# Claiming the tiles of the late chunks' unrounded copies early, and putting the third product ahead of the fourth in two feed-forward units

## The chip, the cores and the metric

The kernel runs on one core of one Trainium2 chip. The metric is the device time of one execution in microseconds (us). Five engines work side by side, each through its own instructions in order: TensorE (PE in the profile, with its weight loads as PEld), VectorE (DVE), ScalarE (ACT), GpSimd (POOL) and SyncE (SP). DMA transfers are issued by the engines' queues; here SP issues plain weight loads, and POOL issues loads that add onto what already lies in the tile.

## The reference

The kernel computes a trunk of two layers for 512 tokens of width 1024, in float32. Layer 0 is a spatial-gating mixer, layer 1 a retention mixer with four heads; behind each mixer stands a SwiGLU feed-forward of hidden width 2816:

```
def swiglu(h, w_gu, w_down):
    a, b = jnp.split(h @ w_gu, 2, axis=-1)
    return (jax.nn.silu(a) * b) @ w_down

for i in range(DEPTH):
    hn = rmsnorm(h, mix_norm_g[i])
    if i % N_MIXERS == 0:
        h = h + sgu_mixer(hn, ...)
    else:
        h = h + retention(hn, positions, ...)
    h = h + swiglu(rmsnorm(h, ffn_norm_g[i]), ffn_w_gu[i], ffn_w_down[i])
return rmsnorm(h, final_norm_g)
```

## The kernel before

**Numbers.** Every float32 product is made of three TensorE products of reduced form (`three`, L246 to L249): high half by high half, low by high, high by low. So each operand is split first. ScalarE writes the rounded high half of a weight tile (`wh_...`, L216), VectorE the remainder (`wl_...`, L223). The raw weights (`wr_...`, 512 KB a tile) come by DMA, from SP (L346) or, added onto a tile, from POOL (L349).

**Products.** The large matrix products use a scheme of seven block products instead of eight (`seven`), named P1, P7, P6, Q4, P5, P2, P3. They add up in three accumulators in PSUM: X takes P1, P6, P5, P3 one after the other, Y takes P7 and then Q4, Z takes P2. PSUM has four slots, handed out in turn. In a feed-forward unit ScalarE copies intermediate states of an accumulator (L1026): X after P1 to `s`, Y after P7 to `y`, X after P6 to `u`. Only after that copy may P5 add onto X. After P5 VectorE adds X to `y`, and only then may P3 go on. Behind Q4 VectorE adds Y to `u`, ScalarE takes its silu, and VectorE multiplies it with `y`; behind P3 VectorE multiplies X with the gated `s`.

**Stages.** Layer 0's mixer (until about 165 us), its feed-forward f0, the retention layer (names ending in `_r`; it starts at about 500 us), and its feed-forward f1 (from about 870 us). A feed-forward is six units of the up and gate product (`gu`), with a first half of the down product (`dn_0`) behind units 0 and 1, and the rest at the end. Tokens come in four chunks of 128. Chunks 2 and 3 are normalised and turned first, and the work of the next stage starts on them; chunks 0 and 1 come late. Of the turned activations the kernel keeps the rounded halves (`XH`, `XL`) and an unrounded copy `xr`, in two pairs of tiles: `XR[name, 1]` for chunks 2 and 3, `XR[name, 0]` for chunks 0 and 1. `raw_copy` writes them on ScalarE (L704) from the accumulator `xT`; sums and differences of them are the operands of P7, P6, P5 and P3 (`xA`: L727, L740, L743). All of these tiles come from one pool of 38 buffers, handed out in the order of the requests.

**Order.** `opened` queues the first four steps of units 0 and 1 in turn with the late chunks' work, and the rest of unit 0 behind them. The order of the products in a unit is a table: FIRST for units 0 and 1, LATER for units 2 to 5 (L314 to L317). The order of the single instructions on each engine is then set by a scheduler that weighs a model of their durations, so a table also moves instructions that it does not name.

Of the kernel before, what the change touches and what calls it, by code (L numbers as in the profile page):

```python
# [8 lines left out]
F32 = mybir.dt.float32  # L9
# [6 lines left out]
P = 128  # L16
# [95 lines left out]
def trunk(ctx, tc, x, positions, mix_g, ffn_g, fin_g, sgu_w_in, sgu_w_s, sgu_b_s, sgu_ln_g, sgu_ln_b,  # L112
          sgu_w_out, ret_w_in, ret_gn_g, ret_w_out, ffn_w_gu, ffn_w_down, invf, decay, out):
    nc = tc.nc
# [9 lines left out]
    H = T // 2  # L124

    def G(name, dtype=F32, shape=(P, 2, T)):
        return gen.tile(list(shape), dtype, tag="g", name=name)
# [10 lines left out]
    def PS(name, shape=(P, 2, T)):  # L138

        s = ps_free.pop(0)  # L140
        t = psp.tile(list(shape), F32, tag=f"ps{s}", name=name)
        ps_held.append((t, s))
        return t

    def done(*tiles):

        for t in tiles:
            i = next(i for i, (u, _) in enumerate(ps_held) if u is t)
            ps_free.append(ps_held.pop(i)[1])
# [102 lines left out]
    X = xpool.tile([P, NC, D], F32, name="X")  # L252
# [60 lines left out]

    ORDER = ("P1", "P7", "P6", "Q4", "P5", "P2", "P3")  # L314
    LATER = ("P1", "P7", "P6", "P2", "P5", "Q4", "P3")
    FIRST = ("P1", "P2", "P7", "P6", "P5", "Q4", "P3")
    SPREAD = ("P1", "P7", "P6", "P2", "Q4", "P5", "P3")  # L317
    BLOCKS = {"P1": ("11",), "P7": ("22", "12"), "P6": ("22", "12", "11"), "Q4": ("22", "12", "11", "21"),
              "P5": ("12", "11"), "P2": ("21",), "P3": ("22",)}
# [2 lines left out]
    def seven(name, w, groups, c1, c2, A, evac, mid=None, look=3, turned=False, order=ORDER, dma=(), onto=(),  # L322
# [10 lines left out]
        chain = {"P1": "X", "P7": "Y", "P6": "X", "Q4": "Y", "P5": "X", "P2": "Z", "P3": "X"}  # L333
# [3 lines left out]
        acc = {}  # L337
# [89 lines left out]
        def run(i):  # L427
            p, (g, s, nk) = order[i // len(steps)], steps[i % len(steps)]
            if apart and p == "P3" and i % len(steps) == 0:
                acc.update({("W", c): PS(f"W{c}_{name}") for c in range(2)})  # L430
            elif p in opens and i % len(steps) == 0:
                acc[chain[p]] = PS(f"{chain[p]}_{name}", (P, wide // P, H) if turned else (P, 2, T))
            if s == 0:
                j = asks.index((p, g))
                for q in asks[j:j + (1 if order is FIRST and p in FIRST[:2] or tied and i == 0 else look)]:
                    A(*q, ask=True)
            n = i % len(steps)
            if p != order[-1]:
                for c in range(2):
                    with tc.issue_after(xn["turned"].ins) if (p, n) in tied and c == 0 else nullcontext():  # L440
                        matmuls(p, g, s, nk, c)
                if n == len(steps) - 1:
                    evac(p, acc, None)
                    if p in closes:
                        done(acc[chain[p]])
            elif n < len(steps) - by_chunk:
                for c in range(2):
                    matmuls(p, g, s, nk, c)
            elif n == len(steps) - 1:
                for c in range(2):  # L450
                    with tc.issue_after(mm.ins) if apart and c == 1 else nullcontext():
                        for st_ in steps[-by_chunk:]:
                            mm = matmuls(p, *st_, c)
                    evac(p, acc, c)
                    if apart:
                        done(acc["W", c])
                if not apart:
                    done(acc["X"])
            if mid and (p, n) in mid:
                mid[p, n]()  # L460

# [233 lines left out]
    XR = {}  # L695

    def raw_copy(name):

        def copy(c, ps):
            if (name, c // 2) not in XR:  # L700
                XR[name, c // 2] = [G(f"xr_{name}_{c // 2}_{j}", F32, (P, 4, H)) for j in range(2)]
            cs = slice((c % 2) * P, (c % 2 + 1) * P)
            for j in range(2):
                nc.scalar.activation(XR[name, c // 2][j][:, :, cs], ps[:, 4 * j:4 * j + 4, :], AF.Copy)  # L704
        return copy
# [296 lines left out]
    def feed_forward(l, ready):  # L1002

        w = ffn_w_gu[l]
        hq = [[None, None] for _ in range(5)]
        he = []
        gates = [None] * 6

        def hidden(u, i):
            gates[u].finish()  # L1010
            return hq[u][i]

        def hidden_end(part, i):
            gates[4].finish()
            gates[5].finish()
            return he[part][i][:, 0:3, :]

        xparts = xA(f"f{l}")

        def unit(u, mid=None, order=LATER, tied=()):  # L1020
            st_ = {}
            n = 2 if u == 5 else 4

            def copy(key, src):
                st_[key] = G(f"{key}_{l}_{u}", F32, (P, 4, H))[:, 0:n, :]
                nc.scalar.activation(st_[key], src, AF.Copy)  # L1026

            def product(i, r, g, ms):
                if u < 4:
                    parts = [(hq[u][i][:, ms, :], ms)]  # L1030
                elif u == 4:
                    parts = [(he[a][i][:, 0:2, :], slice(2 * a, 2 * a + 2)) for a in range(2) if ms.start <= 2 * a < ms.stop]
                else:
                    parts = [(he[a][i][:, 2, :], a) for a in range(2)]
                for dst, ms in parts:
                    nc.vector.scalar_tensor_tensor(dst, r[:, ms, :], -1.0, g[:, ms, :], ALU.mult, ALU.mult)

            def evac(p, acc, c):
                if p == "P7":
                    copy("y7", acc["Y"])  # L1040
                    if u < 4:
                        hq[u][0] = st_["y7"]
                elif p == "P1":
                    copy("s1", acc["X"])
                    if u < 4:
                        hq[u][1] = st_["s1"]
                elif p == "P6":
                    copy("u2", acc["X"])
                elif p in ("Q4", "P2"):
                    a, ps = (st_["u2"], acc["Y"]) if p == "Q4" else (st_["s1"], acc["Z"])  # L1050
                    gates[u] = Chain(lambda: nc.vector.tensor_tensor(a, a, ps, ALU.add),  # L1051
                          lambda: nc.scalar.activation(a, a, AF.Silu),
                          *([lambda: product(0, st_["y7"], a, slice(0, n))] if p == "Q4" else []))
                elif p == "P5":
                    nc.vector.tensor_tensor(st_["y7"], st_["y7"], acc["X"], ALU.add)
                    if u == 5:
                        he.extend([[G(f"he{l}_{a}_{i}", F32, (P, 4, H)) for i in range(2)] for a in range(2)])
                elif p == "P3" and n == 4:
                    product(1, acc["X"], st_["s1"], slice(2 * c, 2 * c + 2))
                elif c == 1:  # L1060
                    product(1, acc["X"], st_["s1"], slice(0, 2))
            first = order is FIRST
            c1, wide = (u * T, T) if u < 5 else (20 * P, 2 * P)
            return seven(f"gu{l}_{u}", w, rows(0, KD), c1, FF + c1, xparts, evac, mid, turned=True, order=order,
                         dma=("P7", "P5") if u == 0 else ("P7",), onto=("P6", "Q4") if u == 0 else ("Q4",) if u < 5 else (),
                         tied=tied, early=0 if u < 5 else 2, wide=wide)

        t = [list(range(4 * u, 4 * u + 4)) for u in range(5)]
        A = [combos(f"h{l}_0", lambda g, i, j: hidden(j, 1 - i), (4,)),
             combos(f"h{l}_1", lambda g, i, j: hidden_end(j, i) if g else hidden(2 + j, i), (4, 3))]  # L1070

        def asks(A):
            return {("P2", 1): lambda: A("P1", 0, ask=True), ("P5", 0): lambda: A("P7", 0, ask=True), ("P3", 1): lambda: A("P6", 0, ask=True)}

        one = unit(0, order=FIRST)
        two = unit(1, {("P7", 1): lambda: A[0]("P1", 0, ask=True), ("P5", 0): lambda: A[0]("P7", 0, ask=True), ("P3", 1): lambda: A[0]("P6", 0, ask=True)},
                   order=FIRST, tied=(("P1", 0),))
        opened(one, two, xparts)
        jobs.extend(two[4:])
        into_x(f"dn{l}_0", ffn_w_down[l], [(t[0], t[1])], A[0], halves=(1, 0))  # L1080
        jobs.extend(unit(2, {**{(p, 0): turn_tables for p in LATER}, ("P3", 1): turn_tables} if l == 0 else None))
        jobs.extend(unit(3))
        jobs.extend(unit(5))
        jobs.extend(unit(4, asks(A[1])))
        into_x(f"dn{l}_1", ffn_w_down[l], [(t[2], t[3]), ([16, 17, 20], [18, 19, 21])], A[1], ready, look=5, apart=ready is finish)
# [157 lines left out]
    t = [list(range(4 * hd, 4 * hd + 4)) for hd in range(HEADS)]  # L1243
    into_x("ro", ret_w_out[0], [(t[0], t[1]), (t[2], t[3])], outA, normed("f1", ffn_g[1:2], raw_copy("f1")),
           {("P1", 1): heads[3][3], ("P7", 1): heads[3][2]})


    feed_forward(1, finish)
    pipeline(jobs)

# [32 lines left out]
```

## Time and profile before

| | |
|---|---|
| device time, median of 3 runs | 1201.62 us (1200.46 to 1202.15) |
| the profiled execution's own time | 1203.81 us |
| its span | 1202.1 us |
| TensorE busy | 1181.7 us (98%), 7158 matmuls |
| VectorE busy | 941.1 us (78%) |
| ScalarE busy | 650.6 us (54%) |
| POOL busy | 163.2 us (14%) |
| DMA traffic | 219.56 MB, 183 GB/s over the span |
| granted TensorE clock, mean | 0.997 |

A row of the timeline has the start in us, the duration in us, the engine, the line of the code, the operation, the tiles written and read, their shapes, and in brackets how long the engine was idle before it and what ended that. Numbers of buffers are left out of names, so `wr_gu_P` is any raw tile of a P product. A duration of a pipelined matmul overlaps that of the next: the spacing of the starts tells what one costs. A row of the windows has the window, its length, then busy time and count of instructions for PE, PEld, DVE, ACT and POOL, the granted clock, the DMA share and the GB/s. A row of the waits has the waiting instruction, what ended the wait, the sum in us, how many times, and the longest.

### The profile page before, as it was taken

How to read it: one execution, taken by the hardware profiler on the slowest of the kernel's cores; microseconds unless marked ns; L12 is line 12 of the kernel's file. 1: busy time of each engine (PE TensorE's matmuls, PEld its weight loads, DVE VectorE, ACT ScalarE, POOL GpSimd, SP SyncE). 2: the span in 40 equal slices, each digit the busy share in tenths (PEclk: the TensorE clock that was granted, in tenths of full speed). 3: DMA queues.
4: the chain of work that ended last, by engine and by line, in shares of the span. 5: the costliest groups of instructions: out<-in, count | busy, mean ns of one | idle time of the engine just before them, and what ended most of it. 6: DMA issues, size and time to landing. Idle time of an engine off the chain costs nothing.

```text
span 1202.1 us, 17966 instructions
## 1 busy us (share of the span) xinstructions
PE 1181.7 (98%) x7158; PEld 1059.7 (88%) x7158; DVE 941.1 (78%) x1119; ACT 650.6 (54%) x821; POOL 163.2 (14%) x145
## 2 busy tenths in 40 slices
PE   8999999999999999999999999999999999999997
PEld 7888899989999987988888888888889989999985
DVE  5587998899977789787665757889787996676897
ACT  5523775554444547555554645576575555535465
POOL 1000122111010130111101011220121110101210
PEclk9999999999999999999999999999999999999999
DMA  9912878898674888767557457778878788856892
GB/s 310 286 41 64 240 160 188 222 233 207 157 204 111 227 177 277 173 145 188 110 167 148 132 128 170 193 145 275 223 159 215 152 228 216 206 128 195 165 246 97
DMA packets 122020, 219.56 MB, mean 183 GB/s; under 512 B 7464, under 2 KB 23888, under 8 KB 121936
## 3 DMA queue, kind: packets, MB, share of 16 engines
q1 hardware_dynamic: 85872, 150.23, 37.7%
q0 software_dynamic: 35776, 67.66, 33.6%
q8 instruction: 56, 0.92, 0.3%
q10 hardware_dynamic: 288, 0.52, 0.1%
q14 instruction: 28, 0.23, 0.1%
HBM read 215.24 MB, written 2.10 MB: 181 GB/s over the span
## 4 chain that ended last, share of the span: by engine, by line
PE 85%; DMA 5%; issue 4%; DVE 2%; ACT 2%; POOL 1%; SPq 0%; DVEq 0%; POOLq 0%; ACTq 0%
PE X_gu L247 6%; PE X_gu L249 6%; PE X_gu L248 6%; PE Y_gu L249 3%; PE Y_gu L248 3%; PE Y_gu L247 3%; DMA wr_gu_P<-in_ffn_w_gu 3%; PE X_dn L247 3%; PE X_dn L248 3%; PE X_dn L249 3%; PE X_vg L248 2%; PE X_vg L247 2%; PE X_vg L249 2%; PE ps_qk L247 2%; PE ps_qk L248 2%
## 5 line engine op out<-in xcount | busy, mean ns | idle before, releaser
L216 ACT ACTIVATE wh_gu_P<-wr_gu_P 128x1024 fp32r<-128x1024 f32 x132 | 135.3, 1053 | 82.2 <-DVE wr_gu_P L377 51.0
L223 DVE TENSOR_TENSOR wl_gu_P<-wr_gu_P,wh_gu_P 128x1024 fp32r<-128x1024 f32 x132 | 158.7, 1221 | 22.2 <-ACT wh_gu_P L216 22.1
L349 POOL DMA_DIRECT2D wr_gu_P<-in_ffn_w_gu x50 | 60.8, 1238 | 411.9 <-DVE wl_gu_P L223 180.0
L216 ACT ACTIVATE wh_dn_P<-wr_dn_P 128x1024 fp32r<-128x1024 f32 x72 | 69.0, 980 | 41.3 <-DMA wr_dn_P<-in_ffn_w_down 17.5
L223 DVE TENSOR_TENSOR wl_vg_P<-wr_vg_P,wh_vg_P 128x1024 fp32r<-128x1024 f32 x48 | 58.5, 1223 | 36.4 <-ACT wh_vg_P L216 30.2
L223 DVE TENSOR_TENSOR wl_dn_P<-wr_dn_P,wh_dn_P 128x1024 fp32r<-128x1024 f32 x72 | 79.7, 1130 | 3.5 <-PE Y_gu L248 2.2
L349 POOL DMA_DIRECT2D wr_vg_P<-in_ret_w_in x26 | 31.5, 1249 | 261.6 <-DMA wr_vg_P<-in_ret_w_in 90.8
L216 ACT ACTIVATE wh_vg_P<-wr_vg_P 128x1024 fp32r<-128x1024 f32 x48 | 49.7, 1055 | 26.7 <-DMA wr_vg_P<-in_ret_w_in 14.6
L349 POOL DMA_DIRECT2D wr_dn_P<-in_ffn_w_down x36 | 41.9, 1200 | 146.5 <-DMA wr_dn_P<-in_ffn_w_down 45.5
L248 PE MATMUL ps_qk<-XL_r,wh_qk 128*128 128x512 f32 (+1 forms) x160 | 55.6, 348 | 0.0
L247 PE MATMUL ps_qk<-XH_r,wh_qk 128*128 128x512 f32 (+1 forms) x160 | 55.4, 349 | 0.0
L249 PE MATMUL ps_qk<-XH_r,wl_qk 128*128 128x512 f32 (+1 forms) x160 | 54.9, 347 | 0.0
L247 PE MATMUL X_gu<-XH_f,wh_gu_P 128*128 128x256 f32 x176 | 50.7, 288 | 2.2 <-ACT xr_f L704 2.2
L247 PE MATMUL Z_gu<-XH_f,wh_gu_P 128*128 128x256 f32 x176 | 50.0, 284 | 1.4 <-DVE s L1051 1.4
L249 PE MATMUL Y_gu<-XH_f,wl_gu_Q 128*128 128x256 f32 x176 | 49.9, 284 | 0.8 <-DVE wl_gu_Q L223 0.8
L249 PE MATMUL X_gu<-XH_f,wl_gu_P 128*128 128x256 f32 x176 | 50.5, 287 | 0.0
L248 PE MATMUL X_gu<-XL_f,wh_gu_P 128*128 128x256 f32 x176 | 50.5, 287 | 0.0
L247 PE MATMUL X_gu<-xP5h_f,wh_gu_P 128*128 128x256 f32 x176 | 49.9, 284 | 0.5 <-ACT u L1026 0.5
L247 PE MATMUL X_gu<-xP6h_f,wh_gu_P 128*128 128x256 f32 x176 | 49.9, 284 | 0.5 <-ACT xP6h_f L740 0.5
L247 PE MATMUL Y_gu<-XH_f,wh_gu_Q 128*128 128x256 f32 x176 | 49.9, 284 | 0.2 <-ACT wh_gu_Q L216 0.2
L249 PE MATMUL Z_gu<-XH_f,wl_gu_P 128*128 128x256 f32 x176 | 49.9, 283 | 0.0
L248 PE MATMUL X_gu<-xP6l_f,wh_gu_P 128*128 128x256 f32 x176 | 49.8, 283 | 0.0
(580 smaller groups left out, 4145.1 us busy)
## 6 DMA issues: line engine op xcount, KB each, us to landing
wr_gu_P<-in_ffn_w_gu SPq DMA_DIRECT2D x110, 512.0 KB, 5.4
wr_gu_P<-in_ffn_w_gu POOLq DMA_DIRECT2D x50, 512.0 KB, 7.2
wr_dn_P<-in_ffn_w_down SPq DMA_DIRECT2D x50, 512.0 KB, 5.1
wr_vg_P<-in_ret_w_in SPq DMA_DIRECT2D x40, 512.0 KB, 4.8
wr_dn_P<-in_ffn_w_down POOLq DMA_DIRECT2D x30, 512.0 KB, 6.9
wr_vg_P<-in_ret_w_in POOLq DMA_DIRECT2D x26, 512.0 KB, 7.2
wr_ro_P<-in_ret_w_out SPq DMA_DIRECT2D x20, 512.0 KB, 5.3
wr_qk<-in_ret_w_in SPq DMA_DIRECT2D x32, 256.0 KB, 3.1
```

What stands on the lines that cost most here:

```text
L216: nc.scalar.activation(h, s, AF.Copy)
L223: nc.vector.tensor_tensor(l, s, f32(h), ALU.subtract)
L247: nc.tensor.matmul(o, ah, bh, start=start, stop=False, skip_group_check=True)
L248: nc.tensor.matmul(o, ah, bl, start=False, stop=False, skip_group_check=True)
L249: return nc.tensor.matmul(o, al, bh, start=False, stop=stop, skip_group_check=True)
L349: nc.gpsimd.dma_start(raw[p, 0, g, s][:, 0:nk, :], source(b, g, s, nk), accum_op=ALU.add)
```

## The change

FIRST gets P3 ahead of Q4. With that, P3 is no longer the last product of units 0 and 1: its gate product is one VectorE operation over 128x1024 instead of two over half of that, Q4 becomes the product that is worked off chunk by chunk, with its add, silu and multiplication once behind the second half, and the request for the down product's P6 operand moves from the end of P3 to the end of Q4. `raw_copy` asks for both pairs of `xr` tiles at its first call in a layer (chunk 3), and POOL writes one column of zeros into each of the two tiles that chunks 0 and 1 will fill. That is done in f0, r and f1: six fills. The values that the fills write are overwritten later.

```diff
-    FIRST = ("P1", "P2", "P7", "P6", "P5", "Q4", "P3")
+    FIRST = ("P1", "P2", "P7", "P6", "P5", "P3", "Q4")
...
                 if not apart:
-                    done(acc["X"])
+                    done(acc[chain[p]])
...
         def copy(c, ps):
-            if (name, c // 2) not in XR:
-                XR[name, c // 2] = [G(f"xr_{name}_{c // 2}_{j}", F32, (P, 4, H)) for j in range(2)]
+            if (name, 0) not in XR:
+                for i in (1, 0):
+                    XR[name, i] = [G(f"xr_{name}_{i}_{j}", F32, (P, 4, H)) for j in range(2)]
+                for t in XR[name, 0]:
+                    nc.gpsimd.memset(t[:, 0, 0:1], 0.0)
...
                 elif p == "P6":
                     copy("u2", acc["X"])
+                elif p == "Q4" and c == 0:
+                    pass
                 elif p in ("Q4", "P2"):
...
-                elif p == "P3" and n == 4:
+                elif c is None:
+                    product(1, acc["X"], st_["s1"], slice(0, n))
+                elif n == 4:
                     product(1, acc["X"], st_["s1"], slice(2 * c, 2 * c + 2))
...
-        two = unit(1, {..., ("P3", 1): lambda: A[0]("P6", 0, ask=True)},
+        two = unit(1, {..., ("Q4", 1): lambda: A[0]("P6", 0, ask=True)},
                    order=FIRST, tied=(("P1", 0),))
```

The order of the instructions moves as follows at the places that the prediction speaks of. In the names, `gu1_0` is unit 0 of f1 and `dn1_0` the first down product of f1, and the last number tells one buffer from another.

The first place is TensorE in f1's unit 0, from P6's last matmuls on. Before:

```order
L247 MATMUL X_gu1_0_8019<-xP6h_f1_8208,wh_gu1_0_P6_0_2_8244 128x256
L248 MATMUL X_gu1_0_8019<-xP6l_f1_8209,wh_gu1_0_P6_0_2_8244 128x256
L249 MATMUL X_gu1_0_8019<-xP6h_f1_8208,wl_gu1_0_P6_0_2_8245 128x256
L247 MATMUL Y_gu1_0_8315<-XH_f1_7855,wh_gu1_0_Q4_0_0_8371 128x256
L248 MATMUL Y_gu1_0_8315<-XL_f1_7856,wh_gu1_0_Q4_0_0_8371 128x256
L249 MATMUL Y_gu1_0_8315<-XH_f1_7855,wl_gu1_0_Q4_0_0_8372 128x256
```

With the change:

```order
L247 MATMUL X_gu1_0_8025<-xP6h_f1_8212,wh_gu1_0_P6_0_2_8248 128x256
L248 MATMUL X_gu1_0_8025<-xP6l_f1_8213,wh_gu1_0_P6_0_2_8248 128x256
L249 MATMUL X_gu1_0_8025<-xP6h_f1_8212,wl_gu1_0_P6_0_2_8249 128x256
L247 MATMUL X_gu1_0_8025<-xP5h_f1_8285,wh_gu1_0_P5_0_0_8280 128x256
L248 MATMUL X_gu1_0_8025<-xP5l_f1_8286,wh_gu1_0_P5_0_0_8280 128x256
L249 MATMUL X_gu1_0_8025<-xP5h_f1_8285,wl_gu1_0_P5_0_0_8281 128x256
```

Q4's matmuls stood between P6 and P5 (32 of them here, 26 in f0's unit 0, 30 and 45 in the two units 1); now none stands there in the two units 0, and two in each unit 1.

The second place is ScalarE in f0's opening, where the turned chunks are rounded and copied. Before:

```order
L671 ACTIVATE XH_f0_1264<-xT_f0_0_1453 128x8x128
L216 ACTIVATE wh_gu0_1_P2_0_2_1447<-wr_gu0_1_P221_0_2_1388 128x1024
L671 ACTIVATE XH_f0_1264<-xT_f0_1_1529 128x8x128
L704 ACTIVATE xr_f0_0_0_1464<-xT_f0_0_1453 128x4x128
L704 ACTIVATE xr_f0_0_1_1465<-xT_f0_0_1453 128x4x128
L216 ACTIVATE wh_gu0_0_P7_0_0_1494<-wr_gu0_0_P722_0_0_1314 128x1024
```

With the change (L707 is what was L704):

```order
L671 ACTIVATE XH_f0_1264<-xT_f0_0_1457 128x8x128
L216 ACTIVATE wh_gu0_1_P2_0_2_1451<-wr_gu0_1_P221_0_2_1392 128x1024
L671 ACTIVATE XH_f0_1264<-xT_f0_1_1531 128x8x128
L216 ACTIVATE wh_gu0_0_P7_0_0_1496<-wr_gu0_0_P722_0_0_1318 128x1024
L707 ACTIVATE xr_f0_0_0_1270<-xT_f0_0_1457 128x4x128
L707 ACTIVATE xr_f0_0_1_1271<-xT_f0_0_1457 128x4x128
```

The rounding of P7's first weight tile has moved ahead of the two unrounded copies. On TensorE, unit 1's P1 (accumulator `X_gu0_1`) has moved ahead of unit 0's P2 (`Z_gu0_0`) there.

The third place is TensorE in f1's first down product, from the end of P2 on. Before:

```order
L248 MATMUL Z_dn1_0_9083<-wl_dn1_0_P2_0_2_8998,h1_0_P2h_0_9003 128x512
L249 MATMUL Z_dn1_0_9083<-wh_dn1_0_P2_0_2_8997,h1_0_P2l_0_9004 128x512
L247 MATMUL X_dn1_0_8962<-wh_dn1_0_P5_0_0_9019,h1_0_P5h_0_9040 128x512
L248 MATMUL X_dn1_0_8962<-wl_dn1_0_P5_0_0_9020,h1_0_P5h_0_9040 128x512
L247 MATMUL Y_dn1_0_9002<-wh_dn1_0_Q4_0_0_9056,h1_0_Q4h_0_9084 128x512
```

With the change:

```order
L248 MATMUL Z_dn1_0_9085<-wl_dn1_0_P2_0_2_9000,h1_0_P2h_0_9005 128x512
L249 MATMUL Z_dn1_0_9085<-wh_dn1_0_P2_0_2_8999,h1_0_P2l_0_9006 128x512
L247 MATMUL Y_dn1_0_9004<-wh_dn1_0_Q4_0_0_9058,h1_0_Q4h_0_9086 128x512
L248 MATMUL Y_dn1_0_9004<-wl_dn1_0_Q4_0_0_9059,h1_0_Q4h_0_9086 128x512
L247 MATMUL X_gu1_2_9242<-XH_f1_7857,wh_gu1_2_P1_0_0_9145 128x256
L248 MATMUL X_gu1_2_9242<-XL_f1_7858,wh_gu1_2_P1_0_0_9145 128x256
L247 MATMUL X_dn1_0_8964<-wh_dn1_0_P5_0_0_9021,h1_0_P5h_0_9042 128x512
```

Two Q4 matmuls of the same product and two P1 matmuls of unit 2 now stand ahead of P5. In the retention layer the third weight tile of P7 (`wh_vg_P7_0_2`) has moved on ScalarE ahead of the rounding of chunk 1 (`XH_r`).

More of the change, by code (lines that the diff above doesn't have):

```diff
@@ L1075, in feed_forward @@
         one = unit(0, order=FIRST)
[L1076 removed]
+        two = unit(1, {("P7", 1): lambda: A[0]("P1", 0, ask=True), ("P5", 0): lambda: A[0]("P7", 0, ask=True), ("Q4", 1): lambda: A[0]("P6", 0, ask=True)},
                    order=FIRST, tied=(("P1", 0),))
```

## The prediction

> **What bounds the kernel now.** I read the first part of the page, then the chain of waits that ended last, then TensorE's waits grouped by what ended them, then its timeline at each of them.
>
> ```profile
> span 1202.1 us, 17966 instructions
> PE 1181.7 (98%) x7158; PEld 1059.7 (88%) x7158; DVE 941.1 (78%) x1119; ACT 650.6 (54%) x821; POOL 163.2 (14%) x145
> PE 85%; DMA 5%; issue 4%; DVE 2%; ACT 2%; POOL 1%; SPq 0%; DVEq 0%; POOLq 0%; ACTq 0%
> ```
>
> TensorE works for 1181.7 of 1202.1 us, and 85% of the last-ending chain is its own matmuls. No matmul is removed. The change can therefore win only what TensorE still idles, and loses every idle microsecond it adds. These are the waits that the touched places hold:
>
> ```profile
> PE xT_in L667 <- DMA X<-in_x: 3.1, 1, 3.1
> PE X_gu L247 <- ACT xr_f L704: 2.2, 1, 2.2
> PE Z_gu L247 <- DVE s L1051: 1.4, 1, 1.4
> ...
> PE Y_gu L249 <- DVE wl_gu_Q L223: 0.8, 1, 0.8
> ...
> PE X_gu L247 <- ACT u L1026: 0.5, 1, 0.5
> ...
> PE Y_vg L249 <- DVE xP7l_r L743: 0.5, 1, 0.5
> ```
>
> The first lies at the start of the program, out of the change's reach. The second is the opening of the second feed-forward layer (f1), the third that of the first (f0), the next two are f0's unit 0, and the last is the opening of the retention layer (r). Together they are 5.4 us: that is nearly all there is to win, apart from the clock, of which more below.
>
> **The change part by part.** *1. Third product ahead of the fourth, f0, unit 0.* P6's last matmul, the first Q4 matmuls and P5's first, on TensorE:
>
> ```profile
> 190.12 0.28 PE L249 MATMUL X_gu<-xP6h_f,wl_gu_P 128*128 128x256 f32 x1
> 190.60 0.38 PE L247 MATMUL Y_gu<-XH_f,wh_gu_Q 128*128 128x256 f32 x1 [0.20 <-ACT wh_gu_Q L216]
> 191.86 0.39 PE L249 MATMUL Y_gu<-XH_f,wl_gu_Q 128*128 128x256 f32 x1 [0.76 <-DVE wl_gu_Q L223]
> ...
> 195.50 0.38 PE L247 MATMUL X_gu<-xP5h_f,wh_gu_P 128*128 128x256 f32 x1 [0.51 <-ACT u L1026]
> ```
>
> ```profile
> 190.50:195.40 4.90, 3.63 (x26) 3.22 (x26) 0.00 (x0) 0.00 (x0) 1.00 1.09 230
> ```
>
> The windows row counts 26 Q4 matmuls between them. Back to back, the matmuls of this shape start 0.12 us apart (the f1 rows of part 3: 901.54 and 901.66), so 26 of them are 3.1 us of the 5.4 from 190.12 to 195.50. The other 2.27 us are the three waits and the slower matmul behind each. The change takes the Q4 matmuls away from here, and P5 stands directly behind P6. But P5 adds onto X, and ScalarE must have copied X to `u` first. The comparison point is P5's start had the Q4 matmuls cost only their own work: 195.50 - 3.12 = 192.38, from which 2.27 has still to come off or be kept. ScalarE's queue:
>
> ```profile
> 187.24 1.05 ACT L1052 ACTIVATE s<-s 128x1024 f32<-128x1024 f32 x1
> 188.19 1.01 ACT L1026 ACTIVATE y<-Y_gu 128x1024 f32<-128x1024 f32 x1
> ...
> 194.45 1.00 ACT L1026 ACTIVATE u<-X_gu 128x1024 f32<-128x1024 f32 x1
> ```
>
> The changed order puts one weight rounding ahead of the `y` copy and one more, with P3's operand, between it and the `u` copy. ScalarE starts its 1024-column operations 0.95 us apart (187.24 to 188.19): four of them from 188.19 put the `u` copy at 191.99, and P5 at 193.05. From TensorE's side, P6 ends 0.6 us later than now (part 2), so the copy ends at 190.12 + 0.6 + 0.28 + 0.05 + 1.0 = 192.05, and P5 starts at 192.1. Against 192.38, parts 1 and 2 in f0's unit 0 are between -0.3 and +0.8 (the high end with the slower first matmul, 0.1). I take **+0.3**, the middle, for neither row decides which queue is later.
>
> *2. f0's opening.* The changed ScalarE order also puts a P7 weight ahead of the two copies to `xr`:
>
> ```profile
> 164.69 1.02 ACT L671 ACTIVATE XH_f<-xT_f 128x1024 fp32r<-128x1024 f32 x1 [0.69 <-PE xT_f L667]
> 165.61 1.08 ACT L704 ACTIVATE xr_f<-xT_f 128x512 f32<-128x512 f32 x2
> 166.57 1.07 ACT L216 ACTIVATE wh_gu_P<-wr_gu_P 128x1024 fp32r<-128x1024 f32 x1
> ```
>
> ```profile
> 167.12 0.36 PE L247 MATMUL Z_gu<-XH_f,wh_gu_P 128*128 128x256 f32 x1 [1.41 <-DVE s L1051]
> ```
>
> The copies then end at 166.57 + 1.08 = 167.65. Unit 1's P1 now stands first on TensorE, in the accumulator that these copies empty, and starts at about 167.7 instead of 167.12: +0.6, which is already inside part 1. The gap grows from 1.41 to 2.0 us.
>
> *3. The other three places where P5 follows P6.* In f1's unit 0 (and, by the orders, f1's unit 1 and f0's unit 1) the Q4 matmuls that stood there hid the copy entirely:
>
> ```profile
> 901.54 0.28 PE L249 MATMUL X_gu<-xP6h_f,wl_gu_P 128*128 128x256 f32 x1
> 901.66 0.28 PE L247 MATMUL Y_gu<-XH_f,wh_gu_Q 128*128 128x256 f32 x1
> ```
>
> P6's last matmul, the copy and P5's first now run one after the other: 0.28 + 0.05 + 1.00 + 0.05 = 1.38 us from start to start (the copy as in its row of f0; 0.05 from its end at 195.45 to P5 at 195.50, taken for both handovers) where 0.12 stood, **+1.26** in f1's unit 0. Each unit 1 keeps two Q4 matmuls between, 0.24 us of cover: **+1.02** in f1 and **+1.02** in f0. I see no way for the copy to be shorter than its row, and nothing else stands between on TensorE, whose order is fixed. Were the copy queued behind another ScalarE operation, each would cost up to 0.95 more.
>
> *4. f1's down-projection after units 0 and 1.* The changed order puts two Q4 matmuls of the down-projection and two of unit 2's P1 between its P2 and its P5. Unit 2's first weights are late for that:
>
> ```profile
> 963.90 0.39 PE L249 MATMUL X_dn<-wh_dn_P,h_P6l 128*128 128x512 f32 x1
> 964.12 0.39 PE L247 MATMUL Z_dn<-wh_dn_P,h_P2h 128*128 128x512 f32 x1
> ...
> 969.34 0.39 PE L249 MATMUL Z_dn<-wh_dn_P,h_P2l 128*128 128x512 f32 x1
> ```
>
> ```profile
> 971.13 1.06 ACT L216 ACTIVATE wh_gu_P<-wr_gu_P 128x1024 fp32r<-128x1024 f32 x1 [2.02 <-DMA wr_gu_P<-in_ffn_w_gu]
> ```
>
> ```profile
> 964.32 0.37 SPq L346 DMA_DIRECT2D wr_gu_P<-in_ffn_w_gu  x1
> ```
>
> ```profile
> wr_gu_P<-in_ffn_w_gu SPq DMA_DIRECT2D x110, 512.0 KB, 5.4
> ```
>
> SyncE issues the load once P6's last matmul has ended (964.32). The weight is rounded from 971.13 to 972.19. TensorE leaves P2 at 969.57 (one spacing of 0.23 behind 969.34), and two matmuls later, at 970.03, waits until about 972.2: 2.2 us, with P5 and all that follows queued behind. At the page's median of 5.4 us a load that starts at 964.32 would be there at 969.7 and the wait would be 0.9 us; had it come before 969, nothing. I take **+2.0**, near this place's own rows, bounds 0 and 2.2.
>
> *5. The early claim.* Six one-column fills on POOL (two in each layer) are the price:
>
> ```profile
> 852.20 1.22 POOL L349 DMA_DIRECT2D wr_gu_P<-in_ffn_w_gu  x1 [44.52 <-DMA wr_gu_P<-in_ffn_w_gu]
> ```
>
> POOL idles 44.52 us ahead of f1's first accumulating load, and works 14% of the span, so the fills cost nothing there. Without that cover each would be bounded by this row's 1.22 us. As to the gain, in f1's opening ScalarE's order is the same as now:
>
> ```profile
> 873.34 1.05 ACT L216 ACTIVATE wh_gu_P<-wr_gu_P 128x1024 fp32r<-128x1024 f32 x1
> 874.28 0.60 ACT L704 ACTIVATE xr_f<-xT_f 128x512 f32<-128x512 f32 x1
> ```
>
> The copy starts 0.94 us behind the weight rounding ahead of it, with no idle in brackets: it waited for its turn, not for a buffer, and I count **0** for the claim here. In r's opening a weight rounding moves up into idle time of ScalarE, ahead of the second turned half, and P7's low half should come in time:
>
> ```profile
> 519.76 0.50 PE L249 MATMUL Y_vg<-wh_vg_P,xP7l_r 128*128 128x512 f32 x1 [0.46 <-DVE xP7l_r L743]
> ```
>
> That is **-0.5** (0 to -0.6).
>
> *6. The remaining edits* (P3's gate product in one operation instead of two, Q4's once instead of never split, the hook moved) change VectorE's work by less than one issue a unit; VectorE is idle 22% of the span and their results are used only by the down-projection, whose P1 and P7 stand ahead. I count 0; without that cover, one of the 0.9 to 1.2 us operations.
>
> Sum: 0.3 + 1.02 + 1.26 + 1.02 + 2.0 - 0.5 = **+5.1 us**. Against the profiled execution's own 1203.81 us (its span of 1202.1 and 1.7 around it) that gives 1208.9; that execution was 2.2 us above the median of the runs, 1201.62, so the forecast is **1206.7**. With every part at its bounds the sum goes from -0.3 + 3.3 + 0 - 0.6 = +2.4 to 0.8 + 3.3 + 2.2 - 0 = +6.3.
>
> **The clock.** One gap cost more than itself:
>
> ```profile
> 877.40:880.80 3.40, 3.40 (x19) 3.40 (x18) 2.86 (x3) 3.39 (x4) 0.13 (x1) 0.50 0.00 0
> ```
>
> A microsecond after f1's 2.2 us gap the granted clock was 0.50 for 3.4 us, in which half the work, 1.7 us, was lost. No such stretch followed f0's gap of 1.41. [...]
>
> **The rivals.** *First, the new gaps drop the clock as f1's did.* f0's opening (2.0 us) and the down-projection (2.2 us) come near the gap that did. For it: that row. Against: one case only, and f0's lost nothing at 1.41. One drop gives 1206.7 + 1.7 = 1208.4, two 1210.1. *Second, unit 2's weight arrives in time,* because the shifted program starts its load earlier or against less traffic. For it: the page's 5.4 us median against some 6.7 here. It takes off 1.1 to 2.0, and with f0 at its low end gives 1204.1 to 1205.6. *Third, the claim does free the openings.* If what delays the `xr` copies in f1 is their buffer, decided before the weight rounding in front of them, f1's gap and its slow stretch go: 5.1 - 2.2 - 1.7 = +1.2, 1202.8. If f0's gap of 1.41 goes as well and unit 2's weight is in time, the sum loses that, part 2's 0.6 and part 4: 1.2 - 1.4 - 0.6 - 2.0 = -2.8, **1198.8**, faster than now. It decides when the copies run before the weight roundings; the unbroken ScalarE rows and the unchanged order at f1 speak against it. That the claim does nothing is part of the forecast.
>
> **How the numbers follow.** Forecast 0.48; clock drops 0.12; weight in time 0.18; f1's opening freed 0.10; both openings freed 0.12. A measurement of this kernel tells 0.2%, 2.4 us, from no change. Slower: 0.48 + 0.12 + half of 0.18 (its low half lies at the bound) = 0.69. Same: 0.09 + 0.10 = 0.19. Faster: 0.12. The likeliest's own range is 1204.0 to 1207.9; to leave out 2 in 10, it goes down to 1200.0, with part of the last case outside, and up to 1209.8, with two clock drops outside.
>
> **What would show it.** Right: in the changed profile waits of some 1.0 us for `u` in four places (three of them new), a wait of up to 2.2 us for `wh_gu_P` in f1's down-projection, the waits for `wl_gu_Q` and `wh_gu_Q` gone, `xr` waits of about 2 us in both openings. Wrong: no `xr` wait at f1 or a granted clock of 1.00 throughout (third rival); `u` waits under 0.5 us; an added slow stretch near 170 or 972 us (first).

## The result

The changed kernel takes 1214.26 us (median of 4 runs, 1213.14 to 1214.98) against 1201.88 us before (1200.46 to 1203.27): a ratio of 1.0100, 95% interval 1.0088 to 1.0113. It is 12.4 us slower. The forecast was 5.1 us slower, 1206.7, at most 1209.8: the direction was right and the size less than half of what came. The profiled execution of the change took 1213.14 us, that of before 1203.81.

The page after, its first two lines, and TensorE's waits grouped by what ended them (sum in us, times, longest):

```profile
span 1211.4 us, 17975 instructions
PE 1183.4 (98%) x7158; PEld 1061.9 (88%) x7158; DVE 941.3 (78%) x1115; ACT 649.6 (54%) x821; POOL 163.7 (14%) x151
```

```profile
PE X_gu L247 <- ACT u L1029: 5.6, 4, 2.7
PE X_gu L247 <- ACT xr_f L707: 4.1, 2, 2.2
...
PE X_gu L247 <- ACT wh_gu_P L216: 3.1, 2, 1.8
...
PE ps_qk L247 <- DVE u L1172: 0.4, 1, 0.4
```

TensorE has the same 7158 matmuls and is busy 1.7 us longer. Of the four waits for `u` three are new (f0's unit 0 had one), and so are the two for unit 2's first weight (`wh_gu_P`); `xr_f` now holds both openings, where f0's wait stood under `s`. The waits for Q4's weights and for `xP7l_r` are gone. In the timeline, in order of time: f0's opening, P5 in f0's unit 1, unit 2's weight in f0's down product, P6's last matmul and P5's first in f1's unit 0, P5 in f1's unit 1, and unit 2's weight in f1's down product:

```profile
167.77 0.39 PE L247 MATMUL X_gu<-XH_f,wh_gu_P 128*128 128x256 f32 x1 [1.97 <-ACT xr_f L707]
223.82 0.39 PE L247 MATMUL X_gu<-xP5h_f,wh_gu_P 128*128 128x256 f32 x1 [0.88 <-ACT u L1029]
264.60 0.38 PE L247 MATMUL X_gu<-XH_f,wh_gu_P 128*128 128x256 f32 x1 [1.25 <-ACT wh_gu_P L216]
903.32 0.28 PE L249 MATMUL X_gu<-xP6h_f,wl_gu_P 128*128 128x256 f32 x1
906.32 0.38 PE L247 MATMUL X_gu<-xP5h_f,wh_gu_P 128*128 128x256 f32 x1 [2.72 <-ACT u L1029]
937.97 0.39 PE L247 MATMUL X_gu<-xP5h_f,wh_gu_P 128*128 128x256 f32 x1 [0.88 <-ACT u L1029]
979.31 0.39 PE L247 MATMUL X_gu<-XH_f,wh_gu_P 128*128 128x256 f32 x1 [1.81 <-ACT wh_gu_P L216]
```

The idle time at each place, in us, from two profiles of before and three of the change (two of these five are the ones shown; the others were taken with the experiments):

| place | before | changed |
|---|---|---|
| f0 opening | 1.4, 1.4 | 2.0, 2.0, 2.0 |
| f0 unit 0, P6 to P5 | 1.5, 2.6 | 1.1, 1.1, 1.1 |
| f0 unit 1, P6 to P5 | 0 | 0.9, 0.9, 0.9 |
| f0 down product, unit 2's weight | 0 | 1.3, 1.1, 1.2 |
| r opening, `xP7l_r` | 0.5, 0.5 | 0 |
| r, `ps_qk` for `u` (L1172) | 0 | 0.4, 0.9, 0.9 |
| f1 opening | 2.2, 2.2 | 2.2, 2.2, 2.2 |
| f1 unit 0, P6 to P5 | 0 | 2.7, 2.5, 3.0 |
| f1 unit 1, P6 to P5 | 0 | 0.9, 0.9, 0.9 |
| f1 down product, unit 2's weight | 0 | 1.8, 1.8, 1.8 |

By the means this is +7.3 us, and the pages agree. The spans of the three profiled executions of the change are 1211.4, 1209.0 and 1213.2 us, those of before 1202.1 and 1201.7: by the means 9.3 us more. TensorE's busy time is 2.0 us of that (1183.5 against 1181.6), and the idle time the other 7.3.

The busy time grew with the clock. In some stretches of 3.41 us the granted clock was 0.50. On both sides of the end of one, at 910.03 us:

```profile
909.02 0.41 PE L248 MATMUL X_gu<-xP5l_f,wh_gu_P 128*128 128x256 f32 x1
909.23 0.41 PE L249 MATMUL X_gu<-xP5h_f,wl_gu_P 128*128 128x256 f32 x1
...
910.30 0.28 PE L249 MATMUL X_gu<-xP5h_f,wl_gu_P 128*128 128x256 f32 x1
910.42 0.28 PE L247 MATMUL X_gu<-xP5h_f,wh_gu_P 128*128 128x256 f32 x1
```

The matmuls start 0.21 us apart at clock 0.50 and 0.12 behind it (medians 0.213 and 0.120 for this shape, at every such stretch between the program's first 20 us and its end, in all profiles of this study). So a stretch in which TensorE never idles costs 3.41 x (1 - 0.120 / 0.213) = 1.5 us by these spacings, not the 1.7 that a clock of 0.50 over 3.41 us comes to. Leaving out the first 20 us and the end of the program, the three profiles of the change hold three, one and three stretches, the two of before one each. That is 1.3 more by the means, or 2.0 us, as much as the busy time grew.

The medians of all runs lie 12.1 us apart (1214.26 over 10 runs of the changed kernel, 1202.11 over 74 of before). The other 2.8 us are open: the profiled executions of before took 1.3 and 1.7 us more than their median, those of the change 1.3 less than theirs by the mean, and no trace shows what the other executions held. One slow stretch more or less would be of that size. The mean granted clock on record, 0.9934 over these 10 runs and 0.9964 over these 74, points the same way but doesn't give the size. It counts the slow start of the program only in some runs: the eight matmuls into `xT_in` from 8.90 us before and from 9.54 us with the change took 1.94 us each time, at a recorded clock of 1.00 in one and 0.50 in the other. And among the 74, the runs at 0.995 and those at 0.997 took the same time, 1202.5 and 1202.4 us by the means.

### The profile page after: what moved, and what is told of

The parts are those of the page before. It is cut to its first block, busy times and chain, and to the rows that moved or that the text cites. A ratio compares the mean times of both kernels' runs of the same rounds, so it can differ in the third digit from the quotient of the medians.

```text
span 1211.4 us, 17975 instructions
## 1 busy us (share of the span) xinstructions
PE 1183.4 (98%) x7158; PEld 1061.9 (88%) x7158; DVE 941.3 (78%) x1115; ACT 649.6 (54%) x821; POOL 163.7 (14%) x151
## 4 chain that ended last, share of the span: by engine, by line
PE 89%; DMA 4%; DVE 3%; ACT 2%; issue 2%; SPq 0%; POOL 0%; DVEq 0%; ACTq 0%; POOLq 0%
PE X_gu L247 7%; PE X_gu L249 7%; PE X_gu L248 7%; PE Y_gu L249 3%; PE Y_gu L248 3%; PE Y_gu L247 3%; PE X_dn L248 3%; PE X_dn L247 3%; PE X_dn L249 3%; PE ps_qk L247 2%; PE ps_qk L249 2%; PE ps_qk L248 2%; PE X_vg L247 2%; PE X_vg L248 2%; PE X_vg L249 2%; DMA wr_gu_P<-in_ffn_w_gu 2%
## 5 line engine op out<-in xcount | busy, mean ns | idle before, releaser
L249 PE MATMUL X_gu<-xP5h_f,wl_gu_P 128*128 128x256 f32 x176 | 50.5, 287 | 0.0
L248 PE MATMUL X_gu<-xP5l_f,wh_gu_P 128*128 128x256 f32 x176 | 50.5, 287 | 0.0
L249 PE MATMUL Y_gu<-xP7h_f,wl_gu_P 128*128 128x256 f32 x176 | 49.8, 283 | 0.0
```

Of the source, the lines that this page charges most:

```text
L248: nc.tensor.matmul(o, ah, bl, start=False, stop=False, skip_group_check=True)
L249: return nc.tensor.matmul(o, al, bh, start=False, stop=stop, skip_group_check=True)
```

## The experiments

**Claim and order apart.** `claim_only` has the new `raw_copy` with the old FIRST, `order_only` the new FIRST with the old `raw_copy`.

```diff
 # claim_only, against the kernel before
-            if (name, c // 2) not in XR:
-                XR[name, c // 2] = [G(...) for j in range(2)]
+            if (name, 0) not in XR:
+                for i in (1, 0):
+                    XR[name, i] = [G(...) for j in range(2)]
+                for t in XR[name, 0]:
+                    nc.gpsimd.memset(t[:, 0, 0:1], 0.0)
```

> The early claim with its fills, the products in the old order. Theory A: f0's opening gap grows from 1.4 to 2.0 us as in the changed kernel (+0.6, and +1.7 where a slow stretch follows), r's opening gains 0.7, unit 0's fourth product still waits: 1201 to 1203 us, no difference that can be measured. Rival B: the claim carries half of the loss, 1206 us or more.

> P3 ahead of Q4 as in the change, but the xr tiles asked for as before, no fills. Theory A, the table's order carries nearly all of the loss: waits for u in four places (5.6 us in sum, 2.7 in f1's unit 0), waits for unit 2's first weight in both down products (1.3 and 1.8), a gap of 1.4 us in f0's opening as before: 1209 to 1212 us. Rival B, the early claim of two more buffers a layer delays the weight loads and carries half or more: at most 1207 us, u waits the same but the waits in the down products gone.

`claim_only` took 1203.22 us, ratio to before 1.0011 (1.0001 to 1.0020); `order_only` 1213.08 us, 1.0091 (1.0074 to 1.0107). The two add up, 1.3 and 10.9 us, to what the whole change costs, and the order carries nine tenths of it. Both medians lie above the ranges expected, by 0.2 and 1.1 us. TensorE's waits in `claim_only`, and then in `order_only`:

```profile
PE X_gu L247 <- ACT xr_f L707: 4.1, 2, 2.2
...
PE X_gu L247 <- ACT u L1029: 1.2, 2, 0.8
```

```profile
PE X_gu L247 <- ACT u L1026: 6.5, 4, 3.0
...
PE X_gu L247 <- ACT wh_gu_P L216: 2.7, 2, 1.5
PE X_gu L247 <- ACT xr_f L704: 2.2, 1, 2.2
PE Z_gu L247 <- DVE s L1053: 1.4, 1, 1.4
```

The longer f0 opening (1.97 us of the 4.1) belongs to the claim, the waits for `u` and for unit 2's weight to the order. That the claim holds back loads and carries half of the loss (rival B) is out: the down products wait without it too. The claim has one cost of its own, the 0.7 us that `ps_qk` waits for `u` in r: `claim_only` has that wait, `order_only` doesn't. And the claim did not shorten f1's opening, for which the third rival of the prediction had hoped.

**Unit 2's weight.** `unit2_tied` moves on TensorE only the two P1 matmuls of unit 2, in each layer, behind P5 of the down product.

```diff
+                    after_ins = xn["turned"].ins if (p, n) in tied and c == 0 else \
+                        xn["dn_mm"].ins if (p, n) == ("P1", 0) and name[:2] == "gu" and name[-2:] == "_2" and c == 0 else None
+                    with tc.issue_after(after_ins) if after_ins is not None else nullcontext():
+                        mm = matmuls(p, g, s, nk, c)
+                    if p == "P5" and name[:2] == "dn":
+                        xn["dn_mm"] = mm
```

> The changed kernel, but unit 2's P1 is not issued before the last P5 matmul of the first down products; on TensorE only these four matmuls (two in each layer) move. Theory A: both waits for wh_gu_P in the down products go (1.3 + 1.8 us, and a slow stretch behind the second in those runs that have it), nothing takes their place, 3 to 4 us less than the changed kernel of the same call: about 1210.5. Rival: the late weight is wanted by something else anyway, or the loads of the down product are late too, and the wait moves behind P5: less than 1 us gained.

It took 1210.04 us, 1.0065 (1.0051 to 1.0079), against 1214.37 of the changed kernel beside it: 4.3 us less. No wait for `wh_gu_P` is left in its list. That is a little above the 3.1 us of idle time and the 3 to 4 expected, which the spread of the runs allows.

**The changed kernel again, and the clock.**

> The changed kernel once more, for its spread and a second profile. Its gaps of TensorE in the first profile were 1.97 us (f0 opening), 2.2 (f1 opening), 2.72 (f1 unit 0), 1.81 (f1 down product), 1.25 (f0 down product); a stretch of 3.4 us at clock 0.50 followed the first three. Theory C, the clock looks at fixed windows of 3.41 us and drops for the next one where TensorE idled more than about half of one: the same gaps come back within 0.2 us, but which of the 1.8 to 2.2 us gaps are followed by a slow stretch changes with where the windows fall, so runs of the same kernel differ by steps of 1.7 us, and 1213 to 1215 us here. Rival: a gap above a fixed length always drops the clock; then the same three gaps are followed by slow stretches again and the fourth never is.

> The changed kernel, a third profile. The first two (1213.1 and 1210.7 us) account for 7.5 us of waits at full clock and 3 us of clock against 12 measured. Theory C: gaps at the same seven places within 0.3 us of the first two, and slow stretches behind those that fill more than about 1.75 us of one window. Rival: another place with more than 1 us of loss that both earlier profiles missed.

These took 1214.37 us (1210.68 to 1215.43; 1.0104, 1.0089 to 1.0119) and 1213.69 us. The gaps came back within 0.3 us at f1's unit 0 and within 0.13 elsewhere, but for `ps_qk` (0.4, then 0.9 twice); the slow stretches did not: three in the first profile, one in the second, three in the third. The windows view (start and end in us, length, PE busy and matmuls, granted clock, DMA share, GB/s) for the first profile of the change, each pair a stretch of 3.41 us and the one behind it, on the grid that the starts of the slow stretches set (169.34, 879.31 and 906.62 us in this profile: 709.97 and 27.31 us apart, 208 and 8 times 3.413):

```profile
165.93:169.34 3.41, 1.57 (x13) 1.00 0.97 253
169.34:172.75 3.41, 3.41 (x18) 0.50 0.18 13
875.90:879.31 3.41, 1.24 (x11) 1.00 0.50 91
879.31:882.72 3.41, 3.41 (x19) 0.50 0.48 151
903.21:906.62 3.41, 0.69 (x6) 1.00 1.11 199
906.62:910.03 3.41, 3.41 (x18) 0.50 1.10 255
978.30:981.70 3.40, 2.39 (x11) 1.00 1.00 225
981.70:985.10 3.40, 3.40 (x16) 1.00 1.10 190
```

And for the second:

```profile
163.99:167.40 3.41, 1.44 (x12) 1.00 1.08 222
167.40:170.81 3.41, 3.41 (x18) 0.50 0.23 87
877.37:880.78 3.41, 1.72 (x14) 1.00 0.70 148
880.78:884.19 3.41, 3.41 (x30) 1.00 0.21 82
```

The gap of f1's opening was 2.17 us in both profiles. In the first it lay whole in one window and a slow stretch followed; in the second only 1.69 us of it fell into the window from 877.37, and none followed. Over all 14 profiles of this study, but for the first 20 us and the end, TensorE idled 1.84 us or more in 18 windows at a clock of 1.00, and each was followed by a window at 0.50 (in the first profile of the change those with 1.84, 2.17 and 2.72 us, in the second the one with 1.97). No window at 1.00 with 1.70 or less was (1.01 in the first, 1.69 in the second); of four between 1.75 and 1.80, one was (1.75 in `order_only`, from 189.18 us, but not 1.79 in `unit2_tied`, from 163.30). In one case (`one_less`, from 905.96) the slow window itself idled 0.8 us and a second slow one followed it. So in these runs the time depended on where the windows fell: behind the same gap of 2.17 us TensorE's work took 1.5 us longer in the first profile and no longer in the second. That is what theory C expected, and the rival (a fixed length of gap) is out.

What a stretch costs the program can be less. In all three profiles of the change P5 in f0's unit 0 starts 25.9 us behind the opening's first matmul, with a stretch between them and a wait of 1.1 us for `u`. In `unit2_tied`, with the same order there and no stretch, it starts 25.4 us behind it, with a wait of 2.1: most of the 1.5 us would have been waited anyway.

**What `u` waits for.** `u_next` asks for P3's weights (their load and their rounding) three steps later and for its operand one product later; `one_less` does only the latter. By `u_next` unit 2's two P1 matmuls also leave their place ahead of P5 in the down products; by `one_less` ten Q4 matmuls of each unit 0 move ahead of P3, behind the place that is read here, so TensorE's order does not stay quite as its expectation says.

```diff
+        if order is FIRST:                     # u_next only
+            behind = {**behind, "P3": 3}
...
-                for q in asks[j:j + (1 if order is FIRST and p in FIRST[:2] or tied and i == 0 else look)]:
+                for q in asks[j:j + (1 if order is FIRST and p in FIRST[:2] or tied and i == 0 else 2 if order is FIRST and p == "P6" else look)]:
```

> The changed kernel, but with P3's weight roundings and P3's operand in units 0 and 1 asked for later, so that in each unit 0 ScalarE copies u directly behind y; by the order the unit 2 matmuls also leave their place ahead of the down products' P5. Theory A, the excess of f1's unit 0 over my 1.26 us came from what ScalarE had queued ahead of u: the waits for u in both units 0 come out at 1.0 to 1.2 us, the one in f1 1.6 shorter and with no slow stretch behind it, those in units 1 stay near 0.9; waits in the down products gone: 1206 to 1208 us. Rival: u waits for TensorE's P6 to be complete in another way, or P3 becomes late and TensorE waits there: the time stays above 1210 us.

> The changed kernel, but P3's operand in units 0 and 1 is asked for one product later; by the order ScalarE's queue between y and u in each unit 0 shrinks from two operations to one, and TensorE's order stays. If each operation queued ahead of u costs 0.95 us (theory A), the wait for u in f1's unit 0 is about 1.8 us: 2.5 to 2.7 with two operations, 1.05 with none. A gap of that size is at the edge where a slow stretch follows (about 1.75 us in one window), so 1 to 2.5 us less than the changed kernel: about 1211.5 us. Rival: u is late for another reason that u_next changed as well (weight loads moved), the wait stays above 2.3 us and the time at 1214.

`u_next` took 1209.60 us, 1.0060 (1.0048 to 1.0072), above the 1206 to 1208 expected. One of its six executions took 4217 us, for a reason that no trace shows; the ratio leaves it out. Its waits for `u` were 1.1 us in each unit 0, as expected, and the slow stretch behind f1's was gone, but a new wait of 0.6 us stood in each down product:

```profile
PE X_gu L247 <- ACT u L1031: 4.1, 4, 1.1
...
PE Z_dn L249 <- DVE h_P2l L508: 1.2, 2, 0.6
```

`one_less` took 1211.63 us, 1.0083 (1.0069 to 1.0097), about as forecast; but for another reason, since its wait in f1's unit 0 was 2.74 us and not 1.8. With one operation fewer ahead of it, `u` was as late as ever. ScalarE in the first profile of the change:

```profile
896.75 2.01 ACT L216 ACTIVATE wh_gu_P<-wr_gu_P 128x1024 fp32r<-128x1024 f32 x2 [4.82 <-DMA wr_gu_P<-in_ffn_w_gu]
...
902.47 1.00 ACT L1029 ACTIVATE y<-Y_gu 128x1024 f32<-128x1024 f32 x1
903.37 1.04 ACT L216 ACTIVATE wh_gu_P<-wr_gu_P 128x1024 fp32r<-128x1024 f32 x1
904.31 1.04 ACT L743 ACTIVATE xP3h_f<-xP_f 128x1024 fp32r<-128x1024 f32 x1
905.26 1.00 ACT L1029 ACTIVATE u<-X_gu 128x1024 f32<-128x1024 f32 x1
```

and in `one_less`:

```profile
898.15 2.01 ACT L216 ACTIVATE wh_gu_P<-wr_gu_P 128x1024 fp32r<-128x1024 f32 x2 [4.91 <-DMA wr_gu_P<-in_ffn_w_gu]
...
905.71 1.01 ACT L1029 ACTIVATE u<-X_gu 128x1024 f32<-128x1024 f32 x1
```

ScalarE stands idle 4.8 us for P6's second weight tile, and then works without a break until `u`. From the landing to `u` are 8.51 us with nine operations in between, 7.56 with eight: one operation is 0.95 us, as theory A had it. But in `one_less` the rounding of the tile began 5.9 us before P6 ended (904.02), in the first profile of the change 6.9 us before (903.60), and that ate the gain. The wait for `u` is thus a load's landing plus a queue, and not a queue that starts when P6 ends.

**The load.** The tile is landed by POOL's accumulating load. In the first profile of the change, and then before:

```profile
wr_gu_P<-in_ffn_w_gu POOLq DMA_DIRECT2D x1, 512.0 KB, 10.1
```

```profile
wr_gu_P<-in_ffn_w_gu POOLq DMA_DIRECT2D x1, 512.0 KB, 6.5
```

The new table also changes SyncE's order: both of P3's tiles come ahead of unit 1's P7 tiles, where they stood in turn. `loads_as_before` puts only the fetches back; on TensorE nine Q4 matmuls, over the four units, move behind P3 by it.

```diff
-        return [Job(lambda i=i: run(i), [(n + early - behind.get(p, 0), step) for n, step in fetch(p, *st_)]
+        return [Job(lambda i=i: run(i), [(n + early - (2 if order is FIRST and p == "P3" else behind.get(p, 0)), step) for n, step in fetch(p, *st_)]
```

> The changed kernel, but P3's raw weights in units 0 and 1 are fetched two steps later, so that SyncE issues unit 1's P7 tiles ahead of them again, as in the kernel before; ScalarE's order is that of the changed kernel. In the changed kernel's profiles the u copy in f1's unit 0 starts 8.5 us behind the landing of P6's second accumulating load (POOL), nine ScalarE operations later, and that load took 9 to 10 us against 6.2 to 6.5 before. Theory A2: the load is slow because unit 1's P7 loads, now behind P3's, run beside it; with SyncE's old order it lands within 7 us and at least 2 us earlier, u is copied right when P6 ends, the wait falls from 2.5 to 3.0 to about 1.1 us, and 2 to 3 us go: about 1211. Rival: the load is as slow as in the changed kernel (9 us or more) for another reason, the wait stays above 2.3 us and the time at 1214.

It took 1213.16 us, 1.0090 (1.0076 to 1.0103). The load took 7.3 us, a little above the 7 expected, and P5 in f1's unit 0 waited 1.11 us, no more than P6's end and the copy. But the 1.6 us went elsewhere:

```profile
PE X_gu L247 <- ACT u L1029: 4.4, 4, 1.6
...
PE X_gu L247 <- DVE y L1060: 3.2, 2, 2.1
```

P3 now waits in both units 0 for VectorE's sum into `y`, behind P5, a wait that the changed kernel does not have. So the order of the loads explains f1's `u` wait (A2 holds on the load and the wait), while my 1211 missed that the wait would move. What slows the accumulating load is not shown. Plain loads that SyncE issues close to it are a likely reason: the next one came 0.1 us behind it in the first profile of the change, 2.5 us behind it before. But the distance to the next one does not settle it: it was 1.1 us in the second profile of the change, where the load took 9.1 us, and 1.0 in `loads_as_before`. Nor is it the order of the products alone: `claim_only` has the old one, and the accumulating load took 8.7 us.

**A version that is faster than both.** If the openings wait for the place of the `xr` copies in ScalarE's queue, they should gain from being asked for ahead of the rounded half of the chunk. `copies_first` does that on top of `claim_only`, `copies_first_no_claim` on the kernel before. `before_again` stands beside them.

```diff
     def turn(c, src, name, more=None):
...
+        if more is not None and c < 2:
+            more(c, ps)
         nc.scalar.activation(xn["h"][:, :, cs], ps, AF.Copy)
         nc.vector.tensor_tensor(xn["l"][:, :, cs], ps, f32(xn["h"][:, :, cs]), ALU.subtract)
-        if more is not None:
+        if more is not None and c >= 2:
             more(c, ps)
```

> The kernel before once more, for a second profile. By the first profiles TensorE's idle and slow time differs between the two kernels by 6.4 us at full clock (f1 unit 0 +2.8, f1 down product +2.1, f0 down product +1.5, two units 1 +1.1 each, f0 opening +0.6, the rest -2.8) and by two slow stretches, 3.4 us. Theory C: the gap at f1's opening comes back at 2.2 us and is followed by a slow stretch or not, 1200 or 1203 us, whatever else is the same. Rival: this profile shows the other waits of before (fourth product in f0 2.3 us, 1.3 near 451 us) much smaller, so that the first profile understated the loss.

> The claim alone, and in addition the two unrounded copies of the late chunks asked for ahead of the rounded half in each turned chunk. By the order, ScalarE in f1's opening then copies right behind the turned chunk, ahead of four roundings. If the openings wait for the copies' place in ScalarE's queue (theory A), f1's gap of 2.2 us and f0's of 1.4 go, no slow stretch can follow, 1197 to 1199 us, faster than before. Rival: TensorE waits there for something else that is as late (a rounded weight, the chunk's low half), and the gap stays above 1.5 us.

> The copies ahead of the rounded half, but the tiles asked for as before, no fills. By the order the copies in f1 stay behind four weight roundings and the copy to s. Theory A: f1's gap stays near 2 us, f0's may close: 1200 to 1202 us. If only the order of copy and rounded half mattered and not the claim, the same time as with the claim.

`before_again` took 1202.31 us (1.0001, 0.9989 to 1.0013), `copies_first` 1200.65 (0.9991, 0.9980 to 1.0001; not to be told from before, and above the 1197 to 1199 expected), `copies_first_no_claim` 1199.54 (0.9978, 0.9970 to 0.9986). In `copies_first` no wait is left in either opening, as expected, but P6 waits for its operand instead, up to 2.8 us, with a slow stretch behind it:

```profile
PE X_gu L247 <- ACT xP6h_f L745: 4.3, 2, 2.8
```

Without the claim the openings keep 1.4 and 1.6 us, and P6 waits less:

```profile
PE Z_gu L247 <- DVE s L1053: 3.0, 2, 1.6
PE X_gu L247 <- ACT xP6h_f L742: 1.5, 2, 0.8
```

The sum is nearly the same, 4.3 and 4.5 us, but in the second the longest of these gaps is 1.6 us and the granted clock was 1.00 in the stretches that hold them (160 to 250 and 870 to 960 us): TensorE was busy 1179.8 us in its profile against 1180.7. My expectation had it the other way round. It is the fastest version of this study, 2.7 us below the kernel before beside it.

**The order with its side effects repaired.** `repaired` is `u_next` without the claim and with the copies first.

> P3 ahead of Q4 with what the runs blamed taken away: no early claim, copies ahead of the rounded half, P3's roundings and operand later (u directly behind y). What must remain, by theory A, are four waits for u of 1.1 us each and small ones for P2's operand in the down products, against the fourth product's wait in f0 (2.3 to 3.4 us) that it removes. Against copies_first_no_claim (1199.5) that is +4.4 + 2 - 2.5: 1202 to 1205 us, so no better than the old order. Rival, the order pays once its side effects are gone: below 1200.

It took 1205.86 us, 1.0036 (1.0024 to 1.0048), just above its range and 6.3 us above `copies_first_no_claim`, which did not run beside it. No slow stretch stood in its profile, and four waits of 0.9 to 1.1 us for `u` remain:

```profile
PE X_gu L247 <- ACT u L1030: 4.1, 4, 1.1
```

With the waits for `h_P2l` and `h_Q4h` in the down products (1.2 and 0.4 us) they are more than the order saves. That they would go if other matmuls stood between P6 and P5 is argued, not run.

## Why the prediction was wrong

Its reading of what bounds the kernel held: TensorE's matmuls did not change, and the loss is the idle time that was added, plus the clock. The profiles lie 9.3 us apart where 5.1 were forecast, and the parts make up the difference of 4.2: f1's unit 0 +1.5, f0's down product +1.2, `ps_qk` +0.7, the clock +2.0, and small errors of -1.2 in sum. By its steps:

- *Parts 1 and 2, f0's opening and unit 0, +0.3.* The opening's gap came out at 1.97 us for a forecast 2.0, and P5 in unit 0 waits 1.1 us where Q4's waits and P5's own had been 1.5 and 2.6 in sum. That is a gain of 0.4 us in idle time by the means, just below the low end of the range given (-0.3).
- *Part 3, P5 behind P6.* The two units 1 came out at 0.9 us of idle time and about 1.0 with the slower first matmul: right. f1's unit 0 was **mis-sized**: 2.7 us of idle time, 2.9 from start to start (906.32 - 903.32 - 0.12), against 1.26. The step that failed is that the copy to `u` starts when P6 ends. In f0 I followed ScalarE's queue up to `u`, in f1 I did not. I named a queue there ("each would cost up to 0.95 more") but left it out of the sum and its bounds. What set it was an accumulating load that took 10.1 us for 6.5, nine ScalarE operations earlier, since the table also changed the order of the loads, which I had not read on SyncE; with that order put back (`loads_as_before`) the wait was 1.1.
- *Part 4, f1's down product, +2.0.* Measured 1.8: right, and with its cause, as `unit2_tied` shows. But f0's has the same four matmuls in its order and waits 1.2 us; I had left it out of the sum altogether.
- *Part 5, the claim at no gain and no cost.* Right for POOL and for f1's opening. r's gain of 0.5 us came, but 0.4 to 0.9 us were lost again further down, where `ps_qk` waits for VectorE; by `claim_only` that is the claim's cost.
- *The clock.* This is the second term that was missed: 2.0 us in the profiles, and perhaps part of the 2.8 that are open. I gave a drop behind the new gaps a chance of 0.12 and kept it out of the sum, though the one gap of that size in the profile had been followed by one. And one costs 1.5 us of TensorE's work and not 1.7. In the 14 profiles, but for the first 20 us and the end, each of the 18 windows at a clock of 1.00 with 1.84 us or more of idle time was followed by one at 0.50.
- *The base.* The sum was made on a profiled execution that held one slow stretch, and set onto the median of runs. The profiles of the two kernels lie 9.3 us apart, the medians 12.1, so a difference read from single profiles does not carry over to medians as it is.

Of the rivals, the first (the gaps drop the clock) came true at f0's opening in all three profiles of the change and at f1's unit 0 in two, though not at the down product, and came on top of the forecast; the second (the weight in time) and the third (the claim frees the openings) did not.

## What to carry to other kernels

A reordering is priced by reading every queue that it changes, the loads' own included, and from the last landing on: an engine that works without a break behind a late load delivers at that landing plus its queue (here 8.51 us for nine operations of ScalarE), whatever TensorE has finished by then. When an accumulator must be copied away before the next product may use it, keep other matmuls between the two (here the waits for `u` with two or none between were 0.9 to 3.0 us). And ask of an idle gap of TensorE what it costs in clock as well. Here every window with 1.84 us or more of idle time was followed by a slow one, which cost up to 1.5 us of TensorE's work; but a gap of 2.17 us had one behind it in one run and none in another, so the cost is an expected value.

## What was not expected of the hardware

The stretches at a granted clock of 0.50 lay on a grid of 3.41 us (those of the first profile of the change 208 and 8 steps apart) whose place against the program differed from run to run: behind the same gap at f0's opening the slow stretch began 1.57, 0.28 and 0.21 us after the gap's end in the three profiles of the change. Leaving out the first 20 us and the end of the program, in the 14 profiles of this study a stretch followed every window at a clock of 1.00 with 1.84 us or more of idle time (18 of 18) and none with 1.70 or less. By the spacings of 0.213 and 0.120 us each cost up to 1.5 us of TensorE's work. The profiled executions of the change with one and with three stretches (1210.68 and 1214.92 us) lie 4.2 us apart, of which 2.2 are TensorE's busy time and 2.0 its idle time.

And an accumulating load of 512 KB from POOL's queue took 10.1 us in the first profile of the changed kernel and 9.1 in the second, with one order of the loads beside it, and 6.2 to 6.5 before or 7.3 in `loads_as_before`, with another (8.7 in `claim_only`).
